# A decoder layer on one core: FFN 2's ring narrowed six units sooner, its first group's blocks loaded there, and two steps of the gate/up stage put elsewhere on DVE

## The chip, the core and the metric

The kernel runs on one core of one Trainium2 chip. The metric is the time of one execution on the device in microseconds (us), and of several runs the median. The engines are named as the profile names them: PE multiplies matrices (PEld loads its weights), DVE is the vector engine, ACT the scalar engine, POOL is GpSimd, SP the engine that here only issues transfers.

## What is computed

One decoder layer in float32 for 256 tokens of width 2048: a half-step SwiGLU FFN, a mixer of two attention branches, and a second half-step FFN, each followed by a LayerNorm of the scaled residual sum.

```python
def _swiglu(x, w_gate, w_up, w_down):
    return (jax.nn.silu(x @ w_gate) * (x @ w_up)) @ w_down
...
        h = _layer_norm(ALPHA * h + 0.5 * _swiglu(h, ffn1_w_gate[l], ffn1_w_up[l], ffn1_w_down[l]),
                        ln1_g[l], ln1_b[l])
        mix = _mixer(h, positions, w_in[l], ...)
        h = _layer_norm(ALPHA * h + mix, ln2_g[l], ln2_b[l])
        h = _layer_norm(ALPHA * h + 0.5 * _swiglu(h, ffn2_w_gate[l], ffn2_w_up[l], ffn2_w_down[l]),
                        ln3_g[l], ln3_b[l])
```

The FFN's inner width is 5632. The weights are read from the chip's main memory once, 454 MB in all.

## The kernel before

**A product in three matmuls.** Each float32 operand is split into a high part, a rounded copy (`S.copy`, an ACT CAST on line 154), and a low part, the rest (a DVE subtraction on line 155). `triple` (lines 208 to 210) adds high x high, high x low and low x high. So each block of weights, 128 x 1024 numbers (two tiles of the inner dimension by 512 columns), is loaded by SP, cast by ACT, subtracted by DVE and used by PE. The pair (high, low) lies in a **ring** of pairs named `wring`; the loaded block in one of four buffers `raw`, or, where it is used more than once, in its own `sraw`.

**Units.** The work on one block is a unit with three steps: load, split, multiply. `unit`, `look` and `advance` say how many units the loads and splits run ahead of the multiplications. For a column of weights over both token blocks (b=0 and b=1, 128 tokens each) the multiplication with b=1 can lag: `lag` units stay in `behind` until `catch_up` runs them. With a lag of 5 the ring has ten pairs, with a lag of 1 six. `set_ring` takes the pairs that were used longest ago out of the ring; their buffers go back to a pool of 41 slots of 4 KB that all larger tiles share (`act_tile`). A tile that gets a slot waits until the last user of the slot is done.

**Gate and up.** In a column of 512 numbers the first 256 are gate, the others up, so 22 columns. The first two are done by `project`, eight units each. The others go in ten groups of two columns by `Hybrid.group`: for the first eight tiles of the inner dimension, seven products ("forms" 1 to 7) take the place of eight, in the order 1, 5, 6, 7, 2, 4, 3. Forms 5, 6 and 4 need sums of two blocks, formed in place in `sraw` by DVE (line 416); form 7's sum is made by an accumulating transfer that POOL issues (line 418). In a **wide** group (two of three) the scheme also takes one more tile on each side; its blocks of half size are `eraw`, and their sums are called **e sums**. A form so has two units of a whole block (s=0, 1) and, in a wide group, a third for e (s=2). The remaining tiles are plain units, p and q, for the two columns. `Seven` and `Extra` make the sums and splits of the activations, named `xs`, `xe` and `xm`, in steps during the first two columns. Of a group's results, Silu (`sg`), some sums (`gus`) and the product (`hb`) are made by `half` and `sum_done`.

**h's way to the down projection.** When both columns of a pair are done, `later(4, ...)` lets `put_h` run four units on: DVE transposes 32 x 32 blocks (line 702, `blocks`), POOL issues four transfers for each of the two token blocks to `hT` in main memory (line 704), and the down projection reads that back. `hb`, `sg`, `gus` and `blocks` share six small buffers (`tmp_tile`).

**FFN 2's start.** The LayerNorm ahead of it finishes its second token block while FFN 2 runs already; so a lag of 5 is set in the last column ahead of FFN 2 (`widen`), and `second(6)` brings it back to 1 in column 1's seventh unit. The rows of that LayerNorm (`z`) are finished by DVE (lines 816 and 817) and stored by POOL (line 1348, `res`) in the same stretch. FFN 1 starts without a lag (`norm` is None there).

**What sets the order.** The program text gives dependences and priorities; the Tile framework's scheduler then lays down each engine's instructions in a fixed order. `tc.issue_after(x)`, used by `behind_split(n)`, forbids it to put an instruction ahead of x: here n counts back over the splits of the groups, so `behind_split(2)` is "not ahead of the last split but one". Each engine runs its order as it stands, and an instruction that waits holds up all behind it; this holds for SP's transfers too.

Of the kernel before, what the change touches and what calls it, by code (L numbers as in the profile page):

```python
# [11 lines left out]
F32 = mybir.dt.float32  # L12
# [6 lines left out]
P = 128  # L19
# [40 lines left out]
def layer_kernel(ctx: ExitStack, tc: tile.TileContext, a: dict, out: bass.AP):  # L60
# [15 lines left out]
    def act_tile(shape, dt=F32, name="act"):  # L76
        return apool.tile(shape, dt, tag="act", name=nm(name), bufs=SLOTS)
# [38 lines left out]
    class Acts:  # L116
        def __init__(self, k, name, kept=()):
            self.name = name
            self.kept = kept
            self.tiles = {}  # L120
            self.ready = set()
            self.made = {}
            self.cast = {}
            self.raws = {}
# [226 lines left out]
    class Hybrid:  # L351


        def __init__(self, x, seven, k_tiles, small=False, extra=None):

            line.clear()
            self.x, self.seven, self.k_tiles, self.small, self.extra = x, seven, k_tiles, small, extra
            self.raws = {n: [act_tile([P, 1024], F32, "sraw") for _ in range(2)] for n in ("11", "12", "22")}
            self.raws["21"] = self.raws["12"] if small else [act_tile([P, 1024], F32, "sraw") for _ in range(2)]
            if extra is not None:  # L360
                for pair in (("11", "12"), ("22", "21")):
                    t = act_tile([P, 2, 512], F32, "eraw")
                    for i, n in enumerate(pair):
                        self.raws[n] = self.raws[n] + [t[:, i, :]]
            self.snaps = [act_tile([P, 2, 512], F32, "snap") for _ in range(2)]

        def group(self, w0, w1, done, wide=False, seeded=False, gates=False):
            banks = {}
            small = self.small
            n2, n3, q5, n1 = [t[:, i, :] for t in self.snaps for i in range(2)]  # L370
            R = self.raws
            blocks = {"11": (w0, 0), "12": (w1, 0), "21": (w0, 2), "22": (w1, 2)}

            plan = {1: ("11", "11", None, "X"), 5: ("12", "11", ("11", "12"), "Z"), 6: ("22", "11", ("11", "22"), "X"),
                    7: (None, "12", ("12", "22"), "X"), 2: ("21", "21", None, "Y"), 4: (None, "11", ("11", "21"), "W"),
                    3: (None, "22", None, "Z")}
            after = {1: lambda: S.copy(n1, banks["X"]), 6: lambda: S.copy(n2, banks["X"]),
                     7: lambda: S.copy(n3, banks["X"]), 5: lambda: S.copy(q5, banks["Z"]),
                     2: lambda: done(0, 0, banks["Y"], n1, ALU.subtract),
                     4: lambda: done(0, 1, banks["W"], n3, ALU.subtract)}  # L380
            stops = {1, 5, 6, 7, 2, 4}

            def bank(n):
                first = n not in banks
                if first:
                    banks[n] = mm_bank()
                return banks[n], first

            def begin():
                S.mul(bank("Y")[0], banks["X"], -1.0)  # L390
            if seeded:
                after[1] = begin
                after[2] = lambda: done(0, 0, banks["Y"], None, None)

            end_s = 2 if wide else 1

            def source(name, s):
                w, j0 = blocks[name]
                if s < 2:
                    return w[j0 + s]  # L400
                i = j0 // 2
                return w[4][:, i * 512:(i + 1) * 512]

            def seventh(p, s):
                load_block, src, add, b = plan[p]
                st = {}
                tiles = G if s < 2 else 1

                def load():
                    nc.sync.dma_start(R[load_block][s], source(load_block, s))  # L410

                def prep():
                    t = R[src][s]
                    if add is not None and (small or p != 7):
                        with nullcontext() if small else behind_split(min(s + 1, 2)):
                            V.tensor_tensor(out=t, in0=t, in1=R[add[1]][s], op=ALU.add)  # L416
                    if not small and p == 6:
                        nc.gpsimd.dma_start(R["12"][s], source("22", s), accum_op=ALU.add)  # L418
                    pair = [v[:, :tiles * 512] for v in next_pair()]
                    split_in_line(not small, *pair, t)  # L420
                    st["pair"] = [v.rearrange("p (g n) -> p g n", g=tiles) for v in pair]

                def now():
                    o, first = bank(b)
                    wh, wl = st["pair"]
                    for g in range(tiles):
                        if s < 2:
                            xh, xl = (v[:, 2 * s + g, :] for v in self.seven.at_[p])
                        else:
                            xh, xl = self.extra.at_[p]  # L430
                        triple(o, xh, xl, wh[:, g, :], wl[:, g, :], first and g == 0,
                               s == end_s and g == tiles - 1 and p in stops, b in "XZ" or seeded)
                    if s == end_s and p in after:
                        after[p]()
                unit(load if load_block else None, prep, now)

            def plain(n, j, last=False):
                w = (w0, w1)[n]
                names = (("Y", "W"), ("Z", "X"))[n]
                st = {}  # L440

                def load():
                    st["raw"] = wpool.tile([P, 1024], F32, tag="raw", name=nm("raw"), bufs=4)
                    nc.sync.dma_start(st["raw"], w[j])

                def prep():
                    pair = next_pair()
                    split_in_line(not small, *pair, st["raw"])
                    st["pair"] = [v.rearrange("p (g n) -> p g n", g=G) for v in pair]

                def now():
                    wh, wl = st["pair"]
                    for b in range(2):
                        o, first = bank(names[b])
                        for g in range(G):
                            k = 2 * j + g
                            triple(o, self.x.at(0, k, b), self.x.at(1, k, b), wh[:, g, :], wl[:, g, :],
                                   first and g == 0, last and g == 1, n == 1 or seeded)
                    if last:
                        with behind_split(1) if gates else nullcontext():  # L460
                            done(1, 0, banks["Z"], n2, ALU.add)
                            done(1, 1, banks["X"], q5, ALU.add)
                unit(load, prep, now)

            end = self.k_tiles // G - 1
            if small:
                order = "15pp6p7p3q2q4qq" if seeded else "1p5p6p7p3q2q4qq"
            elif wide:
                order = "15pp6p72q4q3q"
            elif seeded:  # L470
                order = "15pp6p7p2q4q3qq"
            else:
                order = "1p5p6p7p2q4q3qq"
            turn = {n: iter(range(5 if wide else 4, end + 1)) for n in range(2)}
            for i, c in enumerate(order):
                if c in "pq":
                    plain("pq".index(c), next(turn["pq".index(c)]), i == len(order) - 1)
                else:
                    for s in range(end_s + 1):
                        seventh(int(c), s)  # L480
# [341 lines left out]
    def ffn(n, x, wgu, wdn, residual, g, bt, each, first=None, between=None, nxt=None, cols=None, norm=None):  # L822
# [7 lines left out]
        def half(c, b, up, gate):  # L830
            q = c // 2
            sg = tmp_tile([P, 256], "sg")
            S.activation(sg, gate, AF.Silu)
            if c % 2 == 0:
                hb[b, q] = tmp_tile([P, 512], "hb")
            o = (c % 2) * 256
            V.tensor_tensor(out=hb[b, q][:, o:o + 256], in0=up, in1=sg, op=ALU.mult)
            if c % 2 == 1:
                later(4, lambda: put_h(b, q))

        def gu_done(c, b, bank):
            half(c, b, bank[:, 256:512], bank[:, 0:256])
# [25 lines left out]
        seven = Seven(x.raws)  # L868
        extra = Extra(x, 2)

        def second(j):
            if j == 6:
                lag[0] = 1
                catch_up(1)
                set_ring(6)

        def first_hook(j):
            if first is not None:
# [5 lines left out]
                between=between, norm=norm)  # L884
        project(wgu[1], x, KD, 512, lambda b, bank: gu_done(1, b, bank), hook=second, norm=norm, free=(0, 0))
        look(3, 4)
        hy = Hybrid(x, seven, KD, extra=extra)
        for p in range(1, KF // 4):
            if p == KF // 4 - 1:
                for i, q in enumerate((3, 4, 0)):  # L890
# [558 lines left out]
```

## Time and profile before

| | |
|---|---|
| median of three runs | 1991.75 us (1991.24 to 1992.05) |
| the profiled execution | 1988.12 us, its span 1986.3 us |
| granted clock of PE, mean | 0.997 |
| PE busy | 1966.7 us, 99% |
| DVE busy | 1763.3 us, 89%; in FFN 2's gate/up (1400 to 1700 us) 96% |
| ACT busy | 1259.3 us, 63% |
| read and written | 454.08 and 28.84 MB, 243 GB/s over the span |

The gate/up stage of FFN 1 fills the span's first 450 us, that of FFN 2 about 1280 to 1740. The shares of busy time say which engine has most to do; where PE's pauses lie and what ends them is read from the rows of one stretch. In such a row stand start, duration, engine, line, operation and operands, and in brackets how long the engine sat idle before it and for whom. In a row of a stretch stand its bounds, its length, and for each engine busy time and number of instructions, then PE's clock, the busy share of the DMA engines and GB/s.

### The profile page before, as it was taken

To read this page: it belongs to the slowest core of one execution; us is meant where nothing else is said; L and a number is where in the kernel's file an instruction comes from. 1 tells how busy PE (TensorE), PEld (TensorE's weight loads), DVE (VectorE), ACT (ScalarE), POOL (GpSimd) and SP (SyncE) were. 2 spreads that over 40 slices of the span, in tenths; PEclk is the share of its full clock that TensorE was granted. 3 is DMA by queue.
4 is the path that set the end of the run, shared out by engine and by line. 5 is a ranking of instruction groups with operands and counts; after the bars stand their busy time and mean duration, and the time that the engine had idled before them with its cause. 6 is when DMAs were issued, how large, how long until landed. Compare 5 with 4: busy or idle time off the path is not lost.

```text
span 1986.3 us, 25576 instructions
## 1 busy us (share of the span) xinstructions
PE 1966.7 (99%) x8796; PEld 1621.1 (82%) x8796; DVE 1763.3 (89%) x2143; ACT 1259.3 (63%) x1622; POOL 294.4 (15%) x515
## 2 busy tenths in 40 slices
PE   9999999999999999999999999999999999999997
PEld 7888878788888898888888888877788787888886
DVE  7999999999998889988977686698999999989886
ACT  6676666766655666666667865456666666666551
POOL 0211112112100011002223130012112121121000
PEclk9999999999999999999999999999999999999999
DMA  8978888778777666677667677578788877797763
GB/s 308 290 228 266 277 252 254 219 225 310 260 241 242 206 237 232 229 250 264 216 199 255 219 235 263 174 253 267 242 293 261 241 236 237 215 323 258 244 214 123
DMA packets 144596, 484.64 MB, mean 244 GB/s; under 512 B 20641, under 2 KB 20689, under 8 KB 144465
## 3 DMA queue, kind: packets, MB, share of 16 engines
q1 hardware_dynamic: 112752, 389.60, 57.0%
q0 software_dynamic: 31712, 93.41, 17.7%
q8 instruction: 69, 1.13, 0.2%
q14 instruction: 63, 0.51, 0.1%
HBM read 454.08 MB, written 28.84 MB: 243 GB/s over the span
## 4 chain that ended last, share of the span: by engine, by line
PE 86%; DVE 6%; issue 3%; DMA 2%; ACT 2%; POOL 0%; SPq 0%; DVEq 0%; ACTq 0%; POOLq 0%
PE mm L209 27%; PE mm L210 27%; PE mm L208 27%; DVE wring L155 3%; ACT wring L154 2%; DMA sraw<-in_gu_dram 1%; PE tr L209 1%; PE tr L208 1%; PE tr L210 1%; DVE sraw L416 1%; PE tr L658 0%; DMA raw<-in_gu_dram 0%; DMA sraw<-in_wgm_dram 0%; DVE eraw L416 0%; PE tr L1255 0%
## 5 line engine op out<-in xcount | busy, mean ns | idle before, releaser
L154 ACT CAST wring<-raw 128x1024 fp32r<-128x1024 f32 (+2 forms) x475 | 491.1, 1038 | 351.1 <-PE mm L210 246.8
L155 DVE TENSOR_TENSOR wring<-raw,wring 128x1024 fp32r<-128x1024 f32 (+2 forms) x475 | 568.0, 1201 | 112.0 <-ACT wring L154 109.2
L154 ACT CAST wring<-sraw 128x1024 fp32r<-128x1024 f32 x436 | 451.7, 1051 | 193.8 <-DVE sraw L416 76.8
L155 DVE TENSOR_TENSOR wring<-sraw,wring 128x1024 fp32r<-128x1024 f32 x436 | 522.0, 1220 | 30.0 <-ACT wring L154 26.8
L209 PE MATMUL mm<-wring,h 128*128 128x512 f32 (+2 forms) x1260 | 485.4, 386 | 1.4 <-DVE wring L155 1.2
L210 PE MATMUL mm<-wring,h 128*128 128x512 f32 (+2 forms) x1260 | 485.4, 385 | 0.0
L208 PE MATMUL mm<-wring,h 128*128 128x512 f32 (+2 forms) x1260 | 484.3, 385 | 0.0
L208 PE MATMUL mm<-wring,xs 128*128 128x512 f32 x776 | 303.0, 390 | 2.1 <-ACT wring L154 2.1
L209 PE MATMUL mm<-wring,xs 128*128 128x512 f32 x776 | 303.3, 391 | 1.1 <-DVE wring L155 1.1
L210 PE MATMUL mm<-wring,xs 128*128 128x512 f32 x776 | 302.3, 390 | 0.0
L209 PEld LDWEIGHTS mm<-wring,h 128*128 128x128 f32 x1260 | 236.7, 188 | 51.5 <-DVE wring L155 5.1
L208 PEld LDWEIGHTS mm<-wring,h 128*128 128x128 f32 x1260 | 237.0, 188 | 47.5 <-ACT h L154 0.8
L210 PEld LDWEIGHTS mm<-wring,h 128*128 128x128 f32 x1260 | 236.8, 188 | 46.5 <-DVE h L155 0.7
L416 DVE TENSOR_TENSOR sraw<-sraw,sraw 128x1024 f32<-128x1024 f32 x168 | 199.4, 1218 | 2.8 <-DMA sraw<-in_wdv_dram 1.5
L209 PEld LDWEIGHTS mm<-wring,xs 128*128 128x128 f32 x776 | 145.9, 188 | 34.3 <-DVE wring L155 4.4
L208 PEld LDWEIGHTS mm<-wring,xs 128*128 128x128 f32 x776 | 145.8, 188 | 33.4 <-ACT wring L154 3.2
L210 PEld LDWEIGHTS mm<-wring,xs 128*128 128x128 f32 x776 | 146.0, 188 | 30.0
L209 PE MATMUL mm<-wring,x 128*128 128x512 f32 x348 | 136.2, 391 | 1.8 <-DVE wring L155 1.7
L210 PE MATMUL mm<-wring,x 128*128 128x512 f32 x348 | 135.4, 390 | 0.0
L208 PE MATMUL mm<-wring,x 128*128 128x512 f32 x348 | 135.0, 390 | 0.1
L704 POOL DMA_DIRECT2D hT<-blocks x176 | 96.8, 562 | 177.2 <-DVE blocks L702 177.2
L418 POOL DMA_DIRECT2D sraw<-in_gu_dram x40 | 35.5, 887 | 515.7 <-DVE sraw L416 511.2
(307 smaller groups left out, 2213.4 us busy)
## 6 DMA issues: line engine op xcount, KB each, us to landing
raw<-in_gu_dram SPq DMA_DIRECT2D x167, 512.0 KB, 5.0
sraw<-in_gu_dram SPq DMA_DIRECT2D x160, 512.0 KB, 5.3
raw<-in_dn_dram SPq DMA_DIRECT2D x140, 512.0 KB, 4.6
sraw<-in_gu_dram POOLq DMA_DIRECT2D x40, 512.0 KB, 6.8
sraw<-in_dn_dram SPq DMA_DIRECT2D x36, 512.0 KB, 5.7
hraw<-hT POOLq DMA_DIRECT2D x68, 256.0 KB, 5.0
raw<-in_w_out_dram SPq DMA_DIRECT2D x32, 512.0 KB, 4.4
eraw<-in_gu_dram SPq DMA_DIRECT2D x48, 256.0 KB, 5.8
```

The costliest lines, as they stand in the source:

```text
L154: cast[0] = S.copy(hi, src)
L155: lows[0] = V.tensor_tensor(out=lo, in0=src, in1=hi.bitcast(F32), op=ALU.subtract)
L208: PE.matmul(o, xh, wh, start=first, stop=False, skip_group_check=again)
L209: PE.matmul(o, xh, wl, start=False, stop=False, skip_group_check=again)
L210: PE.matmul(o, xl, wh, start=False, stop=last, skip_group_check=again)
L416: V.tensor_tensor(out=t, in0=t, in1=R[add[1]][s], op=ALU.add)
L418: nc.gpsimd.dma_start(R["12"][s], source("22", s), accum_op=ALU.add)
L704: nc.gpsimd.dma_start(to.rearrange("(g r) (i f) -> i r g f", g=4, i=4)[i], t[32 * i:32 * (i + 1), :].rearrange("r (g f) -> r g f", g=4))
```

## The change

Three edits, all in the gate/up stage; the second and third in both FFNs.

1. In FFN 2 the lag goes to 1 and the ring to six pairs at column 1's first unit (j = 0), not at its seventh. Six of the eight `sraw` tiles of the groups are taken there, and their first blocks are loaded in units 0, 2 and 4; the group's own load of them falls away.
2. `put_h` runs 12 units after the pair is done, not 4.
3. An e sum may stand as early as behind the third split back, where it had to stand behind the second.

```diff
-        def __init__(self, x, seven, k_tiles, small=False, extra=None):
+        def __init__(self, x, seven, k_tiles, small=False, extra=None, early=()):
...
-            self.raws = {n: [act_tile([P, 1024], F32, "sraw") for _ in range(2)] for n in ("11", "12", "22")}
+            self.early = set(early)
+            self.raws = {n: early[n] if n in early else [act_tile([P, 1024], F32, "sraw") for _ in range(2)]
+                         for n in ("11", "12", "22")}
...
+            there, self.early = self.early, ()
...
                 def load():
+                    if s < 2 and load_block in there:
+                        return
                     nc.sync.dma_start(R[load_block][s], source(load_block, s))
...
-                        with nullcontext() if small else behind_split(min(s + 1, 2)):
+                        with nullcontext() if small else behind_split(s + 1):
                             V.tensor_tensor(out=t, in0=t, in1=R[add[1]][s], op=ALU.add)
...
-                later(4, lambda: put_h(b, q))
+                later(12, lambda: put_h(b, q))
...
+        early = {}
+
         def second(j):
-            if j == 6:
+            if j == (6 if norm is None else 0):
                 lag[0] = 1
                 catch_up(1)
                 set_ring(6)
+            if norm is not None and j in (0, 2, 4):
+                name, w, j0 = (("11", 2, 0), ("12", 3, 0), ("22", 3, 2))[j // 2]
+                early[name] = [act_tile([P, 1024], F32, "sraw") for _ in range(2)]
+                for s in range(2):
+                    nc.sync.dma_start(early[name][s], wgu[w][j0 + s])
...
-        hy = Hybrid(x, seven, KD, extra=extra)
+        hy = Hybrid(x, seven, KD, extra=extra, early=early)
```

What it moves on the engines, at three places. First DVE at the start of FFN 2's group 3, where form 5 ends and form 6 begins (L155 is a split, L416 or L421 a sum, L702 or L707 a transpose of h). Before:

```order
L155 TENSOR_TENSOR wring_19_119<-raw_1564_11304,wring_18_118 128x1024
L702 STREAM_TRANSPOSE blocks_1574_11361<-hb_1559_11218 128x512
L702 STREAM_TRANSPOSE blocks_1575_11367<-hb_1563_11263 128x512
L155 TENSOR_TENSOR wring_1408_10093<-raw_1571_11331,wring_1407_10092 128x1024
L416 TENSOR_TENSOR sraw_1507_10685<-sraw_1507_10685,sraw_1511_10689 128x1024
L416 TENSOR_TENSOR sraw_1508_10686<-sraw_1508_10686,sraw_1512_10690 128x1024
L155 TENSOR_TENSOR wring_1406_10091<-sraw_1507_10685,wring_1405_10090 128x1024
L155 TENSOR_TENSOR wring_5_105<-sraw_1508_10686,wring_4_104 128x1024
L416 TENSOR_TENSOR eraw_1515_10693<-eraw_1515_10693,eraw_1516_10694 128x512
L155 TENSOR_TENSOR wring_3_103<-eraw_1515_10693,wring_2_102 128x512
L155 TENSOR_TENSOR wring_21_121<-raw_1577_11383,wring_20_120 128x1024
```

and with the change:

```order
L155 TENSOR_TENSOR wring_1402_10087<-raw_1564_11304,wring_1401_10086 128x1024
L155 TENSOR_TENSOR wring_526_5068<-raw_1571_11331,wring_525_5067 128x1024
L421 TENSOR_TENSOR sraw_1486_10512<-sraw_1486_10512,sraw_1502_10610 128x1024
L421 TENSOR_TENSOR sraw_1487_10513<-sraw_1487_10513,sraw_1503_10611 128x1024
L421 TENSOR_TENSOR eraw_1515_10699<-eraw_1515_10699,eraw_1516_10700 128x512
L155 TENSOR_TENSOR wring_15_115<-sraw_1486_10512,wring_14_114 128x1024
L155 TENSOR_TENSOR wring_1408_10093<-sraw_1487_10513,wring_1407_10092 128x1024
L155 TENSOR_TENSOR wring_1406_10091<-eraw_1515_10699,wring_1405_10090 128x512
L155 TENSOR_TENSOR wring_1404_10089<-raw_1575_11371,wring_1403_10088 128x1024
```

The two transposes are gone from between the plain splits (they stand behind form 7's e split now), and the e sum stands ahead of form 6's first split instead of behind its second. Groups 6 and 9, and FFN 1's groups 3, 6 and 9, change in the same way.

Second, SP's transfers in FFN 2's column 1 (`raw` on L235 is a column's block, on L444 or L449 a group's plain one, `sraw` a group's). Before:

```order
L235 DMA raw_1495_10573<-in_gu2_dram 128x1024
L235 DMA raw_1500_10597<-in_gu2_dram 128x1024
L235 DMA raw_1502_10641<-in_gu2_dram 128x1024
L235 DMA raw_1504_10663<-in_gu2_dram 128x1024
L444 DMA raw_1519_10699<-in_gu2_dram 128x1024
L410 DMA sraw_1507_10685<-in_gu2_dram 128x1024
L410 DMA sraw_1508_10686<-in_gu2_dram 128x1024
L410 DMA sraw_1509_10687<-in_gu2_dram 128x1024
L410 DMA sraw_1510_10688<-in_gu2_dram 128x1024
```

and with the change:

```order
L235 DMA raw_1501_10591<-in_gu2_dram 128x1024
L887 DMA sraw_1486_10512<-in_gu2_dram 128x1024
L887 DMA sraw_1487_10513<-in_gu2_dram 128x1024
L235 DMA raw_1504_10614<-in_gu2_dram 128x1024
L887 DMA sraw_1496_10564<-in_gu2_dram 128x1024
L887 DMA sraw_1497_10565<-in_gu2_dram 128x1024
L235 DMA raw_1507_10634<-in_gu2_dram 128x1024
L235 DMA raw_1508_10653<-in_gu2_dram 128x1024
L887 DMA sraw_1502_10610<-in_gu2_dram 128x1024
L887 DMA sraw_1503_10611<-in_gu2_dram 128x1024
L235 DMA raw_1510_10675<-in_gu2_dram 128x1024
L449 DMA raw_1519_10703<-in_gu2_dram 128x1024
```

The group's six blocks now stand between column 1's blocks of units 3 to 7. `sraw_1503_10611` lies in the slot of `z_1352_9664`, a row of the LayerNorm.

Third, DVE where column 1 begins (`h2_1456_10352` is the last split of the LayerNorm's second token block, `fe`, `fa` and `fb` are Extra's and Seven's sums). Before:

```order
L327 TENSOR_TENSOR fe_1477_10435<-h2raw_1434_10245,fe_1477_10435 128x128
L155 TENSOR_TENSOR wring_5_105<-raw_1486_10488,wring_4_104 128x1024
L155 TENSOR_TENSOR h2_1456_10352<-full_1458_10361,h2_1455_10351 128x512
L327 TENSOR_TENSOR fe_1477_10435<-h2raw_1434_10245,fe_1477_10435 128x128
L816 TENSOR_TENSOR z_1352_9664<-z_1352_9664,gb_1371_9806 128x512
L837 TENSOR_TENSOR hb_1485_10480<-mm_1464_10371,sg_1484_10478 128x256
```

and with the change:

```order
L155 TENSOR_TENSOR h2_1456_10352<-full_1458_10361,h2_1455_10351 128x512
L842 TENSOR_TENSOR hb_1485_10480<-mm_1464_10371,sg_1484_10478 128x256
L287 TENSOR_TENSOR fa_1481_10462<-h2raw_1428_10219,h2raw_1432_10234 128x512
L155 TENSOR_TENSOR xe_1478_10440<-fe_1477_10435,xe_1478_10440 128x512
L339 SCALAR_TENSOR_TENSOR xm_1479_10443<-h2raw_1434_10245,xm_1479_10443 128x128
L287 TENSOR_TENSOR fb_1482_10463<-h2raw_1428_10219 128x512
L287 TENSOR_TENSOR fa_1481_10462<-h2raw_1428_10219,fa_1481_10462 128x512
L155 TENSOR_TENSOR wring_1408_10093<-raw_1488_10516,wring_1407_10092 128x1024
```

Column 1's first split (`raw_1486` before, `raw_1488` now) moved from ahead of that last split to seven rows behind it; its pair is the one of column 0's unit 2. On PE the b=1 products of column 0's units 3 to 6 now follow unit 2's at once, ahead of column 1's first product.

## The prediction

> **What bounds the kernel now.** I read the page's first part, then the stretches around every place where the matrix engine pauses, then the rows of that engine, DVE, ACT and SP there, and last the landing times of the transfers.
>
> ```profile
> span 1986.3 us, 25576 instructions
> PE 1966.7 (99%) x8796; PEld 1621.1 (82%) x8796; DVE 1763.3 (89%) x2143; ACT 1259.3 (63%) x1622; POOL 294.4 (15%) x515
> ...
> 138.00:152.00 14.00, 13.50 (x57) 1.00 0.61 168
> 260.00:274.00 14.00, 13.50 (x57) 1.00 0.63 169
> 383.00:397.00 14.00, 13.43 (x56) 1.00 0.61 166
> 1339.00:1353.00 14.00, 11.11 (x39) 0.88 0.84 260
> 1422.00:1436.00 14.00, 13.41 (x56) 1.00 0.61 170
> 1545.00:1559.00 14.00, 13.52 (x57) 1.00 0.62 168
> 1667.00:1681.00 14.00, 13.43 (x56) 1.00 0.62 162
> ...
> 1560.00:1660.00 100.00, 100.00 (x443) 1.00 0.84 264
> ```
>
> PE is busy 99% of the span, so the span is its work plus its pauses. Busy time hides a pause's full price (a record lasts 0.39 us but a new one starts sooner), so I count matmuls in a stretch. The last row is clean: 443 in 100 us, one every 0.2257 us, hence 62.0 in 14 us. The other rows fall short by 5, 5, 6, 23, 6, 5 and 6. The six small ones are 33 matmuls, **7.4 us**; the large one is 23, **5.2 us**. Together 12.6 us is all that the change can win in these seven places; elsewhere in both gate/up stages PE runs at the clean pace, but for the start of FFN 1 and tenths.
>
> **The six small pauses** stand in groups 3, 6 and 9 of both FFNs (a wide group behind a wide one). One of them, in FFN 2's group 3, on DVE, ACT and PE:
>
> ```profile
> 1421.79 1.22 DVE L155 TENSOR_TENSOR wring<-raw,wring 128x1024 fp32r<-128x1024 f32 x1
> 1422.93 1.30 DVE L702 STREAM_TRANSPOSE blocks<-hb 128x512 f32<-128x512 f32 x2
> 1424.15 1.18 DVE L155 TENSOR_TENSOR wring<-raw,wring 128x1024 fp32r<-128x1024 f32 x1
> 1425.25 2.35 DVE L416 TENSOR_TENSOR sraw<-sraw,sraw 128x1024 f32<-128x1024 f32 x2
> 1427.97 2.36 DVE L155 TENSOR_TENSOR wring<-sraw,wring 128x1024 fp32r<-128x1024 f32 x2 [0.37 <-ACT wring L154]
> 1430.25 0.69 DVE L416 TENSOR_TENSOR eraw<-eraw,eraw 128x512 f32<-128x512 f32 x1
> 1431.62 0.69 DVE L155 TENSOR_TENSOR wring<-eraw,wring 128x512 fp32r<-128x512 f32 x1 [0.69 <-ACT wring L154]
> ...
> 1430.97 0.62 ACT L154 CAST wring<-eraw 128x512 fp32r<-128x512 f32 x1 [0.33 <-DVE eraw L416]
> ...
> 1428.23 0.39 PE L210 MATMUL mm<-wring,h 128*128 128x512 f32 x1
> ...
> 1432.37 0.50 PE L209 MATMUL mm<-wring,xe 128*128 128x512 f32 x1
> 1433.51 0.50 PE L209 MATMUL mm<-wring,h 128*128 128x512 f32 x1 [0.40 <-DVE wring L155]
> 1433.84 0.40 PE L210 MATMUL mm<-wring,h 128*128 128x512 f32 x1
> ```
>
> DVE is late here. It turns h (1.30 us) just before form 6's sums, and the e sum starts only behind both splits, so that ACT casts e at 1430.97, DVE sits 0.69 us waiting for that cast, and PE waits for the low half of e and of the block behind it. From PE's 1428.23 to 1433.84 there are 19 starts in program order: 5.61 - 19 x 0.2257 = 1.32 us lost, nearly all of that stretch's 6 matmuls (1.35); the rest lies at 1422.6, before the transposes, and stays.
>
> **Cost of the transposes and the e sum.** Nothing is added: the same two transposes, the same sum. I put the new order on these rows, with DVE starting an instruction 0.08 us before the last one's end is recorded, as the rows do. Without the transposes the second raw split runs 1422.9 to 1424.1, the two sums to 1426.4, the e sum to 1427.0, the first split to 1428.2, the second to 1429.4 (its cast is ACT's third behind the sums, 1.05 us each), e's to 1430.0. PE asks for the three low halves at 1428.7, 1430.0 and 1431.4 at the clean pace: all three are there. So 1.3 us go in each of six places, **7.7 us**; I take 7.5 for tenths that DVE's new places may cost.
>
> The cover: the transposes now stand behind form 7's e split (wide) or at form 4 (narrow). There DVE has lost none of its lead: the 1.3 us were spent earlier before, so from the new place on it stands as before or earlier, and with PE 1.3 us earlier it had 0.69 + 0.37 us of idle time to give. The e sum holds the first split of forms 4 and 6 back by 0.6 us; it runs ahead of the second split, not of anything more. Without that cover the price is those 0.6 us in 10 such forms. Bounds: 0 to 7.7 us won; a loss is the third rival's.
>
> **The large pause** is FFN 2's first group, form 6.
>
> ```profile
> 1342.23 0.50 PE L208 MATMUL mm<-wring,xs 128*128 128x512 f32 x1 [2.07 <-ACT wring L154]
> 1343.49 0.50 PE L209 MATMUL mm<-wring,xs 128*128 128x512 f32 x1 [0.76 <-DVE wring L155]
> ...
> 1316.13 2.03 SPq L410 DMA_DIRECT2D sraw<-in_gu_dram  x4
> ...
> 1339.70 1.05 ACT L154 CAST wring<-sraw 128x1024 fp32r<-128x1024 f32 x1 [3.46 <-DMA sraw<-in_gu_dram]
> ...
> 1336.71 2.35 DVE L416 TENSOR_TENSOR sraw<-sraw,sraw 128x1024 f32<-128x1024 f32 x2
> 1342.20 1.23 DVE L155 TENSOR_TENSOR wring<-sraw,wring 128x1024 fp32r<-128x1024 f32 x1 [3.14 <-ACT wring L154]
> ...
> 1300.00:1316.00 16.00, 16.00 (x72) 13.00 (x71) 15.93 (x24) 9.65 (x13) 1.64 (x3) 1.00 0.52 159
> 1316.00:1345.00 29.00, 26.17 (x113) 20.99 (x111) 24.67 (x29) 13.09 (x16) 5.14 (x9) 0.98 1.02 348
> ...
> raw<-in_gu_dram SPq DMA_DIRECT2D x9, 512.0 KB, 6.6
> sraw<-in_gu_dram SPq DMA_DIRECT2D x7, 512.0 KB, 11.7
> res<-z POOLq DMA_DIRECT2D x7, 256.0 KB, 6.6
> ...
> raw<-in_gu_dram SPq DMA_DIRECT2D x167, 512.0 KB, 5.0
> ```
>
> The first group's blocks can only be loaded once the ring gives up four pairs, at column 1's unit 6; so SP issues them from 1316.13 on, all at once, and they land 11.7 us later while the DMA engines are full (share 1.02 against 0.52 in the 16 us before). One cast waits 3.46 us for a landing, PE 2.07 and 0.76 us, and the clock of that stretch is 0.88: 0.12 x 14 = 1.7 of the 5.2 us are half speed.
>
> [...]
>
> **Cost of the early ring and loads.** No work is added: the four b=1 half-units of column 0 that were spread over column 1 now run in one piece (4 x 6 x 0.2257 = 5.4 us), and column 1 starts 5.4 us later with six pairs. Six of the eight blocks (3 MB) are issued at column 1's units 0, 2 and 4 and not behind its last one, so in the half-empty stretch. The price is DVE's lead: column 1's first split needs a pair that the burst frees, at about 1300.4; DVE has no wring split to do meanwhile and idles about 0.9 us (the Silu behind its table load). It then carries 16 LayerNorm halves, the sums and splits of Seven and eight column splits:
>
> ```profile
> L155 DVE TENSOR_TENSOR wring<-raw,wring 128x1024 fp32r<-128x1024 f32 x10 | 12.2, 1220 | 0.0
> ...
> L816 DVE TENSOR_TENSOR z<-z,gb 128x512 f32<-128x512 f32 x8 | 5.5, 687 | 0.0
> L817 DVE TENSOR_TENSOR z<-z,gb 128x512 f32<-128x512 f32 x8 | 5.5, 686 | 0.0
> ```
>
> Laid out in the new order (1.14 us a split, 0.60 a half, from start to start), the eight splits end at 1305.1, 1309.1, 1311.2, 1315.2, 1317.0, 1318.7, 1321.5 and 1325.1; PE, with the burst in front, asks at 1306.1, 1309.2, 1311.5, 1315.5, 1317.1, 1319.6, 1322.3 and 1325.2: in time, by 0.1 to 1.0 us. Form 6's first split ends at 1340.8, and PE asks at 1340.4: 0.4 us late. One wait is new on **SP**: the sixth of the early blocks takes the buffer of a LayerNorm row, whose second store is issued about 1312 and lands 6.6 us later, 1318.6 to 1319; behind it on SP's queue stand column 1's last raw block and group 1's first ones. A raw block lands 5.0 us after its issue by the page's median, 6.6 in this stretch, so that last one is there at 1324.7 to 1326.3, and ACT wants it at 1323.8: 0.9 to 2.5 us late, or on time if the store lands sooner. It is nearest to the page's row, since the queue's burst is gone: 0.9. Remainder: 0.4 + 0.9 and two restarts of 0.1, **1.5 us**, between 0 and 5.2. Won: 3.7 us.
>
> **Sum.** 7.5 + 3.7 = 11.2 us. The profiled execution took 1988.1 us (span 1986.3), which gives 1976.9; the runs' median lies 3.6 above that execution, so for the median 1991.75 - 11.2 = **1980.5 us**. Mixer, down projections and the rest of FFN 1 keep their order row for row.
>
> **Rivals.** *First: the first group keeps its pause.* The splits of column 1 are within tenths of what PE asks; if SP's new wait or the smaller ring costs DVE 3 us more, PE stands still in column 1 instead of in form 6. For it: DVE is without a gap from 1307 to 1339. Against it: the load pressure that caused the pause is gone. Won 7.5: 1984.3. *Second: the lateness only moves.* DVE has the same work in less time, and if each of six places gives its 1.3 us back at form 4 or 6, what remains is 3.7: 1988.1, within the measurement. Against it: DVE waits for ACT and free pairs inside every group, so it has leads to spend. *Third, slower: the late transposes hold the small buffers.* The built program makes the next group's hb, sg and gus wait for the stores of the transposed h:
>
> ```profile
> L704 POOL DMA_DIRECT2D hT<-blocks x16: 548/568/597, 1468.1 to 1507.5; - x16
> ...
> DMA to landing us min/median/max: 2.0/4.1/5.7
> ```
>
> Eight issues of 0.57 us behind the first transpose end 5.2 us on, and land at 9.3, at worst 10.9; the narrow group's gus comes on DVE some 10.8 us behind the transposes, its sg half a microsecond later. If landing slips by 0.8 us in the 20 groups, 16 us go: 1991.75 - 11.2 + 16 = 1996.5. From 11.2 / 20 = 0.56 us per group it eats the whole gain. Against it: the median leaves 1.5 us, and wide groups have more.
>
> **Chances.** Forecast 0.74, first rival 0.17, second 0.06, third 0.03. The measurement tells 0.2% (4 us) from no change: the forecast, the first rival and a third of the second are faster, 0.93; the rest of the second is the same, 0.04; slower 0.03. Range: 1977.5 (all 12.6 us give 1979.1; 1.6 less, half of what lies between the median and the profiled execution) to 1987 (4.8 us won: the first rival with a third of the small pauses kept or moved).
>
> **What would show it.** Each of the six stretches, found by its e products, holds 61 or 62 matmuls in 14 us; DVE's e sum stands ahead of the two splits, with no wait of 0.69 us; the first group's 14 us hold 55 or more and the clock there is 1.00; sraw lands in 5 to 7 us. Wrong would be: a wait of PE over 1 us between 1300 and 1345, waits of ACT or DVE for stores of h, or stretches with 56 matmuls that moved to forms 4 or 7.

## The result, and the profile after

The changed kernel takes 1985.73 us in the median of 11 runs (1984.10 to 1988.85), the kernel before 1991.22 us in 11 runs beside it. The ratio is 0.9975, 95% interval 0.9966 to 0.9984: 3.2 to 6.8 us were won, 5.0 in the middle, where 11.2 were forecast.

The page of the changed kernel, its span and its engines:

```profile
span 1982.6 us, 25602 instructions
PE 1961.1 (99%) x8796; PEld 1623.3 (82%) x8796; DVE 1759.4 (89%) x2143; ACT 1258.3 (63%) x1622; POOL 295.0 (15%) x515
```

The same seven stretches as before, found by the e products (bounds, length, PE's busy time and matmuls, clock, DMA share, GB/s), and the mixer:

```profile
138.00:152.00 14.00, 14.00 (x63) 1.00 0.58 179
259.00:273.00 14.00, 14.00 (x63) 1.00 0.61 172
380.00:394.00 14.00, 14.00 (x62) 1.00 0.57 161
1339.00:1353.00 14.00, 8.30 (x30) 0.76 0.50 156
1423.00:1437.00 14.00, 14.00 (x63) 1.00 0.61 172
1544.00:1558.00 14.00, 14.00 (x63) 1.00 0.60 164
1665.00:1679.00 14.00, 14.00 (x62) 1.00 0.57 162
...
800.00:1290.00 490.00, 487.78 (x2220) 1.00 0.68 230
```

The six small pauses are gone: 62 or 63 matmuls where 56 or 57 stood, 62.0 being the clean number. With the 33 missing ones go 33 x 0.2257 = 7.4 us. The large pause has grown: 30 matmuls where 39 stood, 32 x 0.2257 = 7.2 us short in place of 5.2, with the clock at 0.76 in place of 0.88. In the mixer this execution has 2220 matmuls in 490 us and the one before 2232. The order there is the same row for row; the same order with a change behind the mixer alone (e1 below) has 2231. So the number differs between executions of one order, here by 11 matmuls (2.5 us), and the 12 are not put down to the change.

The large pause, on PE, ACT and POOL of the changed kernel:

```profile
1345.02 0.79 PE L208 MATMUL mm<-wring,xs 128*128 128x512 f32 x1 [5.70 <-ACT wring L154]
...
1339.50 1.04 ACT L154 CAST wring<-sraw 128x1024 fp32r<-128x1024 f32 x1 [4.47 <-DMA sraw<-in_gu_dram]
...
1342.98 2.94 ACT L154 CAST wring<-sraw 128x1024 fp32r<-128x1024 f32 x3 [1.95 <-DMA sraw<-in_gu_dram]
...
1331.06 0.90 POOL L423 DMA_DIRECT2D sraw<-in_gu_dram  x1 [3.23 <-PE mm L209]
1332.28 0.86 POOL L423 DMA_DIRECT2D sraw<-in_gu_dram  x1 [0.32 <-ACT wring L154]
...
sraw<-in_gu_dram SPq DMA_DIRECT2D x9, 512.0 KB, 4.7
sraw<-in_gu_dram POOLq DMA_DIRECT2D x2, 512.0 KB, 9.5
```

and the same place of the kernel before (the ACT row at 1339.70 is in the prediction):

```profile
1341.13 1.05 ACT L154 CAST wring<-sraw 128x1024 fp32r<-128x1024 f32 x1
1343.53 1.99 ACT L154 CAST wring<-sraw 128x1024 fp32r<-128x1024 f32 x2 [1.35 <-DMA sraw<-in_gu_dram]
...
1331.14 0.90 POOL L418 DMA_DIRECT2D sraw<-in_gu_dram  x1 [3.28 <-DVE sraw L416]
1332.28 0.86 POOL L418 DMA_DIRECT2D sraw<-in_gu_dram  x1 [0.24 <-PE mm L210]
```

SP's blocks do land sooner, in 4.7 us in place of 11.7. But ACT waits for "sraw<-in_gu_dram" as it did before, and until nearly the same times. Two kinds of transfer bear that name: SP's loads, and the two that POOL issues at 1331.1 and 1332.3, which add block 22 onto block 12 for form 7. Those two leave at the same instant in both kernels (they wait for form 5, which reads block 12), and take 9.8 us before and 9.5 us after, in the median of the two; ACT's casts start when they land, at 1339.5 to 1339.7 and 1343.0 to 1343.5. The blocks that SP loads can't be what ACT waits for at 1339.70: form 6's sums, which read blocks 11 and 22, stand on DVE at 1336.71 already (in the prediction), and form 5's sums, which read block 12, ahead of POOL's transfers. The order of ACT's rows there tells whose casts these are. Before and after:

```
L154 CAST wring_1405_10090<-sraw_1509_10687 128x1024
...
L154 CAST wring_20_120<-sraw_1507_10685 128x1024
L154 CAST wring_4_104<-sraw_1510_10688 128x1024
L154 CAST wring_18_118<-sraw_1508_10686 128x1024
```

```
L154 CAST wring_14_114<-sraw_1496_10564 128x1024
...
L154 CAST wring_1407_10092<-sraw_1497_10565 128x1024
L154 CAST wring_1403_10088<-sraw_1486_10512 128x1024
L154 CAST wring_1401_10086<-sraw_1487_10513 128x1024
```

`sraw_1509`, `sraw_1510` (after: 1496, 1497) is block 12, form 7's; `sraw_1507`, `sraw_1508` (after: 1486, 1487) is block 11, form 6's, which PE needs first. The order on ACT was 7, 6, 7, 6; now it is 7, 7, 6, 6. Before, form 6's first cast stood behind the wait for POOL's first transfer (1341.13); now it stands behind that for the second (about 1343.93, one cast behind 1342.98). That is the theory tested below.

### The profile page after: what moved, and what is told of

Same layout as the page of the kernel before. It is cut to its first block, busy times and chain, and to the rows that moved or that the text cites. A ratio compares the mean times of both kernels' runs of the same rounds, so it can differ in the third digit from the quotient of the medians.

```text
span 1982.6 us, 25602 instructions
## 1 busy us (share of the span) xinstructions
PE 1961.1 (99%) x8796; PEld 1623.3 (82%) x8796; DVE 1759.4 (89%) x2143; ACT 1258.3 (63%) x1622; POOL 295.0 (15%) x515
## 5 line engine op out<-in xcount | busy, mean ns | idle before, releaser
L155 DVE TENSOR_TENSOR wring<-raw,wring 128x1024 fp32r<-128x1024 f32 (+2 forms) x475 | 566.8, 1200 | 116.5 <-ACT wring L154 114.6
L155 DVE TENSOR_TENSOR wring<-sraw,wring 128x1024 fp32r<-128x1024 f32 x436 | 520.6, 1217 | 32.8 <-ACT wring L154 29.1
L421 DVE TENSOR_TENSOR sraw<-sraw,sraw 128x1024 f32<-128x1024 f32 x168 | 198.8, 1214 | 4.1 <-DMA sraw<-in_wdk_dram 1.9
L709 POOL DMA_DIRECT2D turn<-blocks x104 | 56.7, 553 | 169.9 <-DVE blocks L707 107.4
```

The source lines that it names most:

```text
L155: lows[0] = V.tensor_tensor(out=lo, in0=src, in1=hi.bitcast(F32), op=ALU.subtract)
L709: nc.gpsimd.dma_start(to.rearrange("(g r) (i f) -> i r g f", g=4, i=4)[i], t[32 * i:32 * (i + 1), :].rearrange("r (g f) -> r g f", g=4))
```

## The experiments

Theory: PE's large pause comes from the order of ACT's casts, and the early ring and loads made it longer by changing that order. Rivals: the transfers themselves are too late whatever the order; the smaller ring has cost DVE its lead; the other two edits did it. All kernels were timed beside the kernel before; the ratios are to that.

| run | kernel | median us | ratio, 95% interval |
|---|---|---|---|
| e11 | the changed kernel again | 1985.09 | 0.9973, 0.9963 to 0.9983 |
| e1 | changed, form 6's casts first | 1977.53 | 0.9938, 0.9926 to 0.9950 |
| e5 | changed, one row swapped | 1982.63 | 0.9958, 0.9944 to 0.9971 |
| e2 | before + early ring and loads | 1992.98 | 1.0014, 1.0006 to 1.0023 |
| e4 | before, form 6's casts first | 1986.35 | 0.9980, 0.9971 to 0.9989 |
| e3 | before + transposes + e sum | 1980.56 | 0.9952, 0.9940 to 0.9965 |
| e6 | e3, form 6's casts first | 1977.32 | 0.9936, 0.9923 to 0.9948 |
| e8 | before + e sum | 1982.09 | 0.9960, 0.9947 to 0.9972 |
| e9 | e8, form 6's casts first | 1980.38 | 0.9951, 0.9939 to 0.9964 |
| e7 | before + transposes | 1999.16 | 1.0044, 1.0031 to 1.0057 |
| e10 | before + transposes in FFN 1 alone | 1986.69 | 0.9981, 0.9972 to 0.9990 |
| e12 | e7, form 6 first in all of FFN 2 | 1977.08 | 0.9932, 0.9918 to 0.9946 |

**The order of the casts, in the changed kernel (e1) and in the kernel before (e4).** One edit to both; in e1 it changes nothing in the built order but ACT's rows in that one group (the four casts, and one copy by one row), in e4 the casts, and one of SP's loads by one row.

```diff
+            banks, six = {}, [None]
...
-                    split_in_line(not small, *pair, t)
+                    with tc.issue_after(six[0].ins) if first7 and p == 7 else nullcontext(): split_in_line(not small, *pair, t)
+                    six[0], st["pair"] = cast[0], [v.rearrange("p (g n) -> p g n", g=tiles) for v in pair]
...
-                     p % 3 != 1, p > 1)
+                     p % 3 != 1, p > 1, first7=p == 1 and norm is not None)
```

> The changed kernel with one order changed: in FFN 2's first group ACT casts form 6's two blocks ahead of form 7's two. Theory 'order of the casts': PE's pause of 6.1 us at 1338.9 is form 6's split standing on ACT behind form 7's casts, which wait for POOL's accumulating transfers (issued at 1331.1 and 1332.3, landed 1339.4 and 1342.9). With the casts in PE's order at most 1 us of it stays, PE's clock stays 1.00 and the 14 us behind 1339 hold 57 to 62 matmuls in place of 30: 6 to 7.5 us less than the changed kernel, about 1979 us, ratio to before 0.993 to 0.995. Rival 'the transfers themselves': PE needs form 7 so soon that it waits for the landing anyway, the pause moves to form 7 and at most 2 us are won: 1984 us, ratio 0.996. Rival 'early ring': DVE's lead is gone, form 6's split stays late, ratio 0.997 as the changed kernel.

> The kernel before with ACT's order alone changed in FFN 2's first group: form 6's two casts ahead of form 7's. Theory 'order of the casts': 4 to 5 of the 5.2 us go without any earlier load, clock 1.00, ratio 0.9975 to 0.998. Rival 'late loads' (the prediction's reading of the pause): the blocks loaded from 1316 on are what the cast waits for, and nothing changes, ratio 1.000.

The first group's stretch of e1:

```profile
1339.00:1353.00 14.00, 13.49 (x58) 1.00 0.87 271
```

its rows on ACT:

```profile
1338.23 3.13 ACT L154 CAST wring<-sraw 128x1024 fp32r<-128x1024 f32 x3 [0.79 <-DVE sraw L421]
1343.33 1.05 ACT L154 CAST wring<-sraw 128x1024 fp32r<-128x1024 f32 x1 [1.97 <-DMA sraw<-in_gu_dram]
```

and the stretch of e4:

```profile
1342.00:1356.00 14.00, 12.42 (x52) 1.00 1.00 338
```

In e1 ACT casts form 6 right behind its sums (1338.23) and waits for the second transfer only behind that, where it holds up nobody for long: 58 matmuls in place of 30, clock 1.00, 7 to 8 us less than the changed kernel (7.4 by the two ratios, 8.2 by the two medians). The second of POOL's transfers lands as late as ever (the cast that waits for it starts at 1343.33, in the changed kernel at 1342.98; the two take 9.6 us in the median, there 9.5), so their slowness alone does not make the pause. In e4, with SP's blocks as late as before (12.3 us to landing), the same order brings 0.2% (4.0 us, 2.2 to 5.8) of the pause's 5.2: the late blocks were not what most of the pause was made of. Both came out as the theory said.

**The early ring and loads alone (e2), and the other two edits alone (e3).** e3 is the kernel before with the first of these diffs, e2 the changed kernel with the second. (Where the expectations have the e sum "behind the second split back", the edit allows it behind the third, as it stands in the section on the change.)

```diff
-                        with nullcontext() if small else behind_split(min(s + 1, 2)):
+                        with nullcontext() if small else behind_split(s + 1):
...
-                later(4, lambda: put_h(b, q))
+                later(12, lambda: put_h(b, q))
```

```diff
-                        with nullcontext() if small else behind_split(s + 1):
+                        with nullcontext() if small else behind_split(min(s + 1, 2)):
...
-                later(12, lambda: put_h(b, q))
+                later(4, lambda: put_h(b, q))
```

> The kernel before with the early ring and the six early blocks alone (h's transposes and the e sum as before). The prediction's term: 3.7 us won, ratio 0.998. Theory 'order of the casts': ACT's order here is 7, 7, 6, 6 where before it was 7, 6, 7, 6, so the pause grows from 5.2 to about 8 us: 2.9 us slower than before, ratio 1.0015. Rival 'the six places do it': the lost 2.9 us come from the late transposes or the e sum, and this kernel wins the 3.7.

> The kernel before with the other two parts: h's transposes 12 units behind and the e sum behind the second split back; ring and loads as before. The prediction's term: 7.5 us won, 1983.7 us, ratio 0.996; the traces of the two kernels say 8.5 us in the two stages, ratio 0.9957. The pause of FFN 2's first group stays as before (38 to 40 matmuls in its 14 us). So this kernel would be faster than the full change by about 3 us. Rival 'it all hangs together': without the early ring the late transposes give part back, under 5 us won.

The first group in e2, then in e3:

```profile
1343.00:1357.00 14.00, 8.37 (x25) 0.76 0.61 173
```

```profile
1337.00:1351.00 14.00, 11.21 (x41) 0.88 0.71 237
```

Alone, the early ring and loads make the kernel slower, by 0.06 to 0.23%; ACT's order in e2 is 7, 7, 6, 6. The two other edits alone win 9.6 us (7.0 to 11.9), and their first group has kept the pause of before, and ACT's order of before. So the full change is e3's gain, less 4 to 5 us that the first edit costs beside it (4.6 by the ratios). Why the scheduler answers the early ring and loads with another order on ACT, no run shows.

**One row swapped (e5).** The changed kernel with the edit of e1 for form 7's second block alone, behind form 6's first: 7, 6, 7, 6, as before.

```diff
+                    with tc.issue_after(six[0].ins) if first7 and p == 7 and s == 1 else nullcontext(): split_in_line(not small, *pair, t)
+                    six[0], st["pair"] = cast[0] if s == 0 and p == 6 else six[0], [v.rearrange("p (g n) -> p g n", g=tiles) for v in pair]
```

> The changed kernel with one row swapped on ACT: form 6's first cast ahead of form 7's second, which is the order of the kernel before (7, 6, 7, 6); early ring and loads stay. Theory 'order of the casts': the pause is as long as before's, 3.2 us with 38 to 40 matmuls in its 14 us in place of 30, so about 3 us less than the changed kernel: ratio to before 0.9955 to 0.9965. Rival 'early loads': their contention or the smaller ring made the pause grow, and the swap changes nothing: ratio 0.9975.

```profile
1337.00:1351.00 14.00, 10.54 (x31) 0.76 0.60 181
```

The time came out as expected (0.9958), the stretch didn't: PE's wait fell to 2.7 us, but in the profiled execution the mean clock is as low as in the changed kernel (0.76), now with PE busy for 10.54 of the 14 us (there 8.30), and they hold 31 matmuls and not 38 to 40. From 1300 to 1400 us both executions hold 405, so what this one is faster by doesn't lie here. Its ratio speaks for the order, but only weakly, since its interval overlaps the changed kernel's by a little; its profile leaves open how much of the wait comes back as a low clock. The theory rests on e1, e4 and e6.

**All but the early ring and loads (e6).** e3 with the edit of e1; the built order also moves a few other rows of that stretch by some places, among them two matmuls.

> The kernel before with the late transposes, the e sum put back and ACT's order in the first group (form 6's casts ahead of form 7's), without the early ring and loads. If the early loads are worth nothing once the order is right: 0.993 to 0.9938, as the changed kernel with that order (0.9938). If they are worth what the prediction paid for (3.7 us, or the 1.4 us that the stretch behind 1338.5 shows between the two kernels with the order put right, 2.6 against 1.3 us lost): 0.9945 or more.

```profile
1338.00:1352.00 14.00, 12.69 (x56) 1.00 1.00 353
```

0.9936 beside 0.9938: once the casts stand right, the early ring and loads are worth nothing that these runs can tell.

**The transposes alone (e7), the e sum alone (e8), and e8 with the casts (e9).** Each is one of the two edits of e3; e9 adds the edit of e1.

```diff
-                later(4, lambda: put_h(b, q))
+                later(12, lambda: put_h(b, q))
```

```diff
-                        with nullcontext() if small else behind_split(min(s + 1, 2)):
+                        with nullcontext() if small else behind_split(s + 1):
```

> The kernel before with h's transposes 12 units behind alone. By the prediction's layout DVE is 1.3 us earlier in each of six places and e's split, still behind the sum and the cast, ends 0.4 us before PE asks: 6 to 7.7 us won, ratio 0.9962 to 0.997. If the e sum is what makes PE wait: 4 us, 0.998.

> The kernel before with the e sum behind the second split back alone. DVE's 0.69 us of waiting for the cast of e goes in each of six places, the 1.3 us of the transposes stay: 0.6 to 0.7 us won per place, 3.5 to 4.5 us, ratio 0.998. If the transposes alone are the lateness: nothing, 1.000; if the e sum alone is: 7 us, 0.9965.

> The kernel before with two rows of order alone: the e sum put back, and form 6's casts ahead of form 7's on ACT in FFN 2's first group. If h's late transposes and the early ring and loads are worth little: 0.9935 to 0.9945 (0.996 for the e sum, 4 to 5 us for the casts). If the late transposes carry a part of the gain, as the stretches of the e-sum kernel say (2.9 us lost per stage against 1.9 and 1.5 with both): 0.9945 to 0.995.

The e sum alone wins 8.0 us (5.6 to 10.5), where 3.5 to 4.5 were expected; what came out is the expectation's other case, that the e sum alone is the lateness (7 us). The six stretches of the small pauses hold 60 to 62 matmuls, so 28 of the 33 missing ones are back. Its rows on DVE in FFN 2's group 3:

```profile
1421.23 1.30 DVE L702 STREAM_TRANSPOSE blocks<-hb 128x512 f32<-128x512 f32 x2
...
1423.56 2.35 DVE L416 TENSOR_TENSOR sraw<-sraw,sraw 128x1024 f32<-128x1024 f32 x2
1425.83 0.68 DVE L416 TENSOR_TENSOR eraw<-eraw,eraw 128x512 f32<-128x512 f32 x1
1426.43 2.35 DVE L155 TENSOR_TENSOR wring<-sraw,wring 128x1024 fp32r<-128x1024 f32 x2
1428.70 0.68 DVE L155 TENSOR_TENSOR wring<-eraw,wring 128x512 fp32r<-128x512 f32 x1
```

The transposes still stand ahead of form 6, and DVE has no wait behind them (before: 0.37 and 0.69 us): their 1.3 us were lead that DVE had. What PE waited for was the low half of e and of the block behind it, which came late because e's sum, and so its cast, came late. The late transposes alone made the kernel 0.44% slower, which neither expectation had. All of it lies in FFN 2:

```profile
138.00:152.00 14.00, 14.00 (x64) 1.00 0.61 172
1421.00:1435.00 14.00, 13.37 (x57) 1.00 0.69 163
...
1400.00:1700.00 300.00, 294.90 (x1269) 1.00 0.80 246
```

FFN 1's group 3 is clean, and there the built order moved the e sum between form 6's splits; in FFN 2, 300 us hold 1269 matmuls (before: 1303). ACT and DVE of e7 in that group 3, and two rows from where its group 6 begins:

```profile
1428.57 4.15 ACT L154 CAST wring<-sraw 128x1024 fp32r<-128x1024 f32 x4 [1.08 <-DVE sraw L416]
1432.62 1.14 ACT L154 CAST wring<-eraw 128x512 fp32r<-128x512 f32 x2
...
1430.80 0.68 DVE L416 TENSOR_TENSOR eraw<-eraw,eraw 128x512 f32<-128x512 f32 x1
1433.27 0.69 DVE L155 TENSOR_TENSOR wring<-eraw,wring 128x512 fp32r<-128x512 f32 x1 [0.48 <-ACT wring L154]
...
1541.02 0.41 ACT L833 ACTIVATE sg<-gus 128x256 f32<-128x256 f32 x1
1541.46 0.42 DVE L837 TENSOR_TENSOR hb<-gus,sg 128x256 f32<-128x256 f32 x1 [2.92 <-ACT sg L833]
```

The e sum is done at 1431.48, between the two splits. But ACT casts four whole blocks in a row, form 6's and form 7's (6, 7, 6, 7), and form 6's e only behind them at 1432.62, so DVE waits. It is the same thing as in the first group, on a smaller scale, and it says why nothing was won here (57 matmuls, before 56). It doesn't say where the loss lies: the three stretches of groups 3, 6 and 9 hold only 2 matmuls fewer than before, the rest of the 300 us 32 fewer. The largest piece is at 1535 to 1550, with 55 matmuls where 66 would be clean. There DVE sits 2.92 us for a Silu that stands on ACT behind casts which wait 3.08 us for PE and 0.82 us for a load, and PE then waits 0.50 us for ACT and 1.23 us for DVE. That again is a row held up behind others on ACT. A smaller piece is the e sum itself: in form 4 of FFN 2's six wide groups the built order of e7 has it behind both splits (group 3: at 1448.41), where the kernel before has it between them in all six and e12 in five. How the loss divides between the two, these runs don't show.

e9 won less than its first expectation, and lies at the edge of its second. Its first group is nearly whole (56 matmuls from 1339 to 1353, clock 1.00), yet its median is only 1.7 us under e8's, where the stretch promised 4 to 5. The two intervals overlap for the most part, so what the late transposes are worth beside e sum and casts (e6 against e9, 3.1 us by the medians) stays between nothing and a few microseconds.

**The transposes in FFN 1 alone (e10), and with all of form 6 ahead of form 7 in FFN 2 (e12).** e10 has the first line, the kernel before otherwise; e12 is e7 with the edit of e1 and the second line.

```diff
-                later(4, lambda: put_h(b, q))
+                later(12 if norm is None else 4, lambda: put_h(b, q))
...
-                     p % 3 != 1, p > 1)
+                     p % 3 != 1, p > 1, first7=norm is not None)
```

> The kernel before with h's transposes 12 units behind in FFN 1 alone; FFN 2 as before. There the built order puts the e sum between the two splits, in FFN 2 of the kernel with both late it stays behind them. Theory 'the place of the e sum decides': 3.6 us won (5.8 to 2.2 us lost in groups 3 to 9), ratio 0.998. Rival 'late transposes cost by themselves': slower than before, above 1.001.

> The kernel with h's late transposes alone (1.0044), with one rule more: in every group of FFN 2, ACT casts all of form 6 (its e block too) ahead of form 7. In its group 3 ACT had form 7's two casts ahead of the cast of form 6's e, and DVE waited 0.48 us for that. Theory 'order of the casts, there too': the first group's pause (5 us) and most of the 7.2 us lost in groups 3 to 9 go: 1985 to 1989 us, ratio 0.997 to 0.9995. Rival 'late transposes cost DVE by themselves': the first group alone is won, about 1994.5 us, ratio 1.002.

e10 won 3.8 us (2.0 to 5.6), as expected, though the expectation's reason for FFN 2 was only partly right: in e7 form 4's e sum stands behind both splits there, but in form 6 of group 3 it stands between them, and it is e's cast that is late. e12 went beyond what either theory gave it, and is the fastest of all. The stretches of e12:

```profile
1421.00:1435.00 14.00, 14.00 (x64) 1.00 0.64 205
1300.00:1400.00 100.00, 98.10 (x429) 1.00 0.85 278
1400.00:1700.00 300.00, 299.79 (x1320) 1.00 0.83 255
```

and group 3 on ACT:

```profile
1422.81 0.62 ACT L154 CAST wring<-eraw 128x512 fp32r<-128x512 f32 x1 [0.75 <-DVE eraw L416]
1423.34 2.00 ACT L154 CAST wring<-sraw 128x1024 fp32r<-128x1024 f32 x2
```

e is cast as soon as its sum is there, ahead of form 7. From 1269 to 1320 matmuls are 51 x 0.2257 = 11.5 us, of the 22 between e7 and e12; from 1300 to 1400 us, where the first group lies, e12 has 429 matmuls and e7 409, another 4.5 us, and the rest lies around these stretches. Note that the new rule also moved many other rows of PE, DVE and ACT (the e sum stands elsewhere in some groups), so e12 shows that the built order was the cost, not that the casts were all of it.

**The changed kernel again (e11)**, beside e9 and e10:

> The changed kernel itself, beside the two others on the same chip: 0.9975 as first measured, 0.997 to 0.998.

It confirms the first result. e12, e6 and e1 (0.9932 to 0.9938, intervals that overlap) beat it and the kernel before; e12 needs neither the early ring and loads nor the e sum's new place.

## Why the prediction was wrong

- **The six small pauses.** Right in sum: 7.5 us were forecast, 7.4 are counted in the stretches, e3 measured 9.6 (7.0 to 11.9). Wrong in the split, so the sum was in part luck. The working gave the 1.3 us to the transposes and let the e sum help; the e sum alone wins 8.0, with the transposes where they were. The step that failed is "DVE is late here. It turns h (1.30 us) just before form 6's sums": two causes in one row of events, and the longer one was given the price. That the late transposes would have won nothing with the e sum where it was is not shown: in e7, e10 and e12, which have the late transposes without the e sum's edit, the built order put form 6's e sum of groups 3, 6 and 9 between the splits wherever the transposes are late.
- **The cost of the early ring and loads.** This is where the 6 us are that the forecast has too much: 3.7 us won became 4 to 5 us lost, and e3's 2 us above its 7.5 hide a part of that. The step that failed is the reading "One cast waits 3.46 us for a landing", put down to SP's loads issued at 1316.13. The landing was that of POOL's accumulating transfers, which bear the same names; form 6's casts stood behind the waiting one on ACT. The edit left those transfers where they were (1331.1, 1332.3) and turned ACT's order from 7, 6, 7, 6 to 7, 7, 6, 6. With the casts in PE's order the first group's stretch is 4 matmuls short with the early ring and loads (e1, 0.9 us) and 6 without (e6, 1.4 us), and the two times can't be told apart: so it was not the price of the early loads that was off, but the reason to expect a gain from them. That ACT's order there had changed could be read before the run; the text ahead of the prediction compares the orders of DVE, SP and PE.
- **DVE's lead in column 1.** Right, within half a microsecond: up to the large pause PE waits once, 0.4 us, for DVE. It is the split of column 1's last raw block, for which 0.9 us were forecast. SP's new wait is there (2.6 us), but over at 1315, where the working had 1318.6 to 1319; ACT waits for the block and casts it at 1322.11. The row behind it is the group's first plain block, and the 0.88 us there are no part of the forecast:

```profile
1322.11 1.06 ACT L154 CAST wring<-raw 128x1024 fp32r<-128x1024 f32 x1 [2.55 <-DMA raw<-in_gu_dram]
1324.05 1.05 ACT L154 CAST wring<-raw 128x1024 fp32r<-128x1024 f32 x1 [0.88 <-DMA raw<-in_gu_dram]
```

- **The rivals.** "The first group keeps its pause" came nearest (1984.3), and even that is 1.4 us under the measured 1985.7, since the pause grew; its mechanism, column 1 running late, was not what happened. That the measured time lies inside the stated range is luck in this sense: the range reached so far for a rival that did not occur. "The lateness only moves" is out: the six stretches are full. "The late transposes hold the small buffers" didn't occur in the changed kernel: no wait of ACT or DVE in FFN 2's groups is put down to a store of h. A price of the late transposes did exist, 0.44% in e7, of another kind; with the e sum in its new place it is not there (e3 is 18.6 us faster than e7 by the medians). The prediction priced the edits one by one, on rows that each of them re-orders.
- **The clock.** The prediction counts 1.7 us of the large pause as half speed. With a wait of 1.3 us (e6) the clock of the 14 us was 1.00, with waits of 2.07 and 0.76 us (before) 0.88: see the last section.

## What to carry to other kernels

When a wait is put down to a transfer, find which transfer: queue, issue time and landing, not the name alone; here two kinds with one name led to the wrong engine. On an engine that runs its rows as they stand, an early need behind a late one pays the late one's wait (form 6's first cast: at about 1343.93 behind form 7's in the changed kernel, at 1338.23 ahead of them in e1, with a longest wait of PE there of 5.7 us and of 0.3 us), so compare the order of that engine with the order in which its results are needed, before and after a change. Edits that a scheduler answers with a new order don't add up: one and the same line cost 8.8 us alone, and beside another edit nothing that could be told (e3 against e8, 1.5 us faster by the medians, with intervals that overlap).

## What was not expected of the hardware

The two accumulating transfers of 512 KB from POOL took 9.5 us to land in the median in that stretch, where SP's plain loads of the same size took 4.7 in the changed kernel; over its whole execution the page's medians are 5.3 us for SP's 160 loads of `sraw` and 6.6 us for POOL's 40 accumulating ones. Whether it is the adding or POOL's queue that takes longer, no run shows.

PE's clock: taken by single microseconds from 1338 to 1352, the granted clock is 1.00 or, in the low stretch, 0.50 (1344 to 1347 before, 1342 to 1348 after; 0.66 to 0.99 in the microseconds at its edges). With a wait of 1.3 us (e6) it stayed at 1.00; with 2.07 and 0.76 us, before, a stretch of 14 us has a mean of 0.88, that is 0.12 x 14 x 2 = 3.4 us at half speed; with 5.70 us, after, 0.76, that is 6.7 us; and with 2.7 us, in e5, also 0.76. So in these runs the low stretch is not in proportion to the wait. It begins late: about 2.5 us into the pause in the changed kernel, and before only at 1344, when PE was at work again (its second wait ended at 1343.49). The waits of PE in e6, then the longest in e5 (total, times, longest):

```profile
PE mm L208 <- ACT snap L377: 1.3, 1, 1.3
```

```profile
PE mm L208 <- ACT wring L154: 2.7, 1, 2.7
```
